# Half of the k-blocks of the second MLP product by Strassen's method, and the first product in three 256-column passes

## The chip, the cores and the metric

The kernel runs on one core of one Trainium2 chip. The metric is the device time of one execution in microseconds (us); the median of the runs counts. The engines are named as the profile names them: PE (TensorE matmuls), PEld (its weight loads), DVE (VectorE), ACT (ScalarE), POOL (GpSimd), SP (the queue that issues the DMAs).

## The reference

256 tokens (SEQ) of width 2048 (D_MODEL) go through two layers. Layer 0 mixes tokens by forgetting attention, layer 1 by a spatial gating unit; behind each stands a channel MLP of width 8192 (D_FF):

```python
def squared_relu_mlp(h, w1, w2):
    a = jax.nn.relu(h @ w1)
    return (a * a) @ w2
...
    for i in range(DEPTH):
        h = rmsnorm(x, g_mix[i])
        ...
        h = rmsnorm(x, g_mlp[i])
        x = x + squared_relu_mlp(h, mlp_w1[i], mlp_w2[i])
```

Everything is float32. The change is in the MLP of both layers.

## The kernel before

Every large product is made of float32r matmuls in three parts: an operand is split into hi (a cast to float32r) and lo (the rest), and hi·hi, hi·lo and lo·hi are added up in PSUM. The activations lie in SBUF as such pairs: H for the input of a product from x, A for the hidden values. The weights come in a stream of half-chunks of [128, 1024] float32 (512 KB), listed in `halves` in the order of use; each is one step of matmul work, listed in `steps`. For each half-chunk SP issues a DMA into `w_stage` (`load`), ACT casts it to `w_hi` (`split_hi`, L65), and DVE subtracts to get `w_lo` (`split_lo`, L73). The order on all engines is written out by hand: in iteration i of the main loop the half-chunk i+8 is loaded, i+4 is cast, i+3 is split, step i is multiplied, and then what `at(i, ...)` has put behind step i is emitted.

The MLP goes in four rounds (c) of 2048 hidden features. A round has two parts:

- The first product, 16 chunks of 128 features (`chunk_w`; the first two in `pair_w`). A chunk is two steps. For each of 16 k-blocks `mm_w` issues two matmuls with weights as the stationary operand: w_hi times H's hi and lo side by side, 512 columns (L122), and w_lo times H's hi, 256 columns (L124). The two halves of the bank are added and squared in `relu2` (L513 on ACT, L514 and L515 on DVE), and split into A (L206 on ACT, L207 on DVE).
- The second product, four units (n) of 512 output columns (`unit_x`), eight steps each. A step has two k-blocks, two blocks of 128 tokens (t) and three parts: 12 matmuls of 512 columns, with A stationary and the weights moving (L107 to L109). `residual` adds the result to x, scaled by r² per token (L220).

PSUM has four banks under the name `acc` and four under `aux`. POOL makes r, the reciprocal root of the norm (L178).

## Time and profile before

| what | value |
|---|---|
| runs | 2141.71, 2141.81, 2142.49 us; median 2141.81 |
| span of the profiled execution, first to last instruction | 2139.4 us, 2.4 below the median of the runs; the page lists no other time for it |
| PE busy | 2130.9 us, 10428 matmuls |
| PE weight loads | 1770.2 us |
| DVE busy | 1232.4 us (58%) |
| ACT busy | 953.2 us (45%) |
| DMA | 399.38 MB, mean 187 GB/s |

Matmul rows overlap, since the end of a matmul is modelled and the next one starts before it: the time that a matmul takes of PE is read from start to start, not from its duration. An instruction on DVE or ACT also starts a little before the one ahead of it has ended where nothing keeps it waiting.

### The profile page before, as it was taken

The page shows a single profiled execution, that of the slowest core. Times are in us where ns is not written, and L with a number is a line of the kernel's source. Part 1 is how long each engine was busy: PE and PEld are TensorE (multiplying, and loading weights), DVE is VectorE, ACT ScalarE, POOL GpSimd, SP SyncE. Part 2 cuts the span into 40 slices and gives each one's busy share as a digit, 9 for nine tenths or more (in the row PEclk, how much of TensorE's full clock was granted, in tenths as well). Part 3 has the DMA queues.
Part 4 walks back from the last instruction along what each step waited for, and adds up shares of the span by engine and source line. Part 5 has one row for each costly group of instructions (what it writes and reads, how often), then busy time and mean ns, then how long its engine had stood idle before and what let it go on. Part 6 is the DMA issues. An engine that isn't in the chain of part 4 may idle for free.

```text
span 2139.4 us, 26750 instructions
## 1 busy us (share of the span) xinstructions
PE 2130.9 (100%) x10428; PEld 1770.2 (83%) x10428; DVE 1232.4 (58%) x1499; ACT 953.2 (45%) x1308; POOL 55.8 (3%) x41
## 2 busy tenths in 40 slices
PE   9999999999999999999999999999999999999999
PEld 6888888888888888888888888888888888888887
DVE  5665665566456456546555676466556655654653
ACT  6535444444344334434454355454434434433442
POOL 1110110000000000000000000000000000000000
PEclk9999999999999999999999999999999999999999
DMA  7555555556656555555556656555555565564563
GB/s 291 187 166 187 157 169 176 179 192 200 197 160 204 187 176 180 195 182 190 189 188 196 210 175 208 174 165 189 197 177 184 191 206 168 184 215 161 188 217 109
DMA packets 111359, 399.38 MB, mean 187 GB/s; under 512 B 12384, under 2 KB 13040, under 8 KB 110848
## 3 DMA queue, kind: packets, MB, share of 16 engines
q1 hardware_dynamic: 109440, 393.40, 56.6%
q0 software_dynamic: 640, 2.17, 0.4%
q10 hardware_dynamic: 1152, 2.10, 0.3%
q8 instruction: 82, 1.34, 0.3%
q14 instruction: 45, 0.37, 0.1%
HBM read 395.50 MB, written 2.11 MB: 186 GB/s over the span
## 4 chain that ended last, share of the span: by engine, by line
PE 98%; DVE 1%; DMA 0%; POOL 0%; ACT 0%; SPq 0%; issue 0%; DVEq 0%; POOLq 0%; ACTq 0%
PE acc L122 25%; PE acc L108 19%; PE acc L107 19%; PE acc L109 19%; PE acc L124 13%; PE aux L239 0%; DMA w_stage<-in_fox_in 0%; PE aux L408 0%; POOL r_qk L178 0%; PE aux L612 0%; PE aux L437 0%; PE aux L486 0%; DVE qk_sq L401 0%; PE aux L476 0%; ACT qk_nat L391 0%; DVE qk_sq L393 0%
## 5 line engine op out<-in xcount | busy, mean ns | idle before, releaser
L73 DVE TENSOR_TENSOR w_lo<-w_stage,w_hi 128x1024 fp32r<-128x1024 f32 (+1 forms) x738 | 875.9, 1224 | 151.1 <-PE acc L108 121.1
L65 ACT CAST w_hi<-w_stage 128x1024 fp32r<-128x1024 f32 (+1 forms) x738 | 747.1, 1046 | 414.0 <-PE acc L109 377.4
L122 PE MATMUL acc<-H,w_hi 128*128 128x512 f32 x2304 | 814.5, 397 | 0.0
L124 PE MATMUL acc<-H,w_lo 128*128 128x256 f32 x2304 | 648.5, 281 | 0.0
L122 PEld LDWEIGHTS acc<-H,w_hi 128*128 128x128 f32 x2304 | 432.5, 188 | 106.7
L107 PE MATMUL acc<-w_hi,A 128*128 128x512 f32 x1280 | 507.3, 396 | 0.0
L108 PE MATMUL acc<-w_lo,A 128*128 128x512 f32 x1280 | 506.2, 395 | 0.0
L109 PE MATMUL acc<-w_hi,A 128*128 128x512 f32 x1280 | 506.1, 395 | 0.0
L124 PEld LDWEIGHTS acc<-H,w_lo 128*128 128x128 f32 x2304 | 434.3, 189 | 0.4
L109 PEld LDWEIGHTS acc<-w_hi,A 128*128 128x128 f32 x1280 | 240.4, 188 | 58.1
L108 PEld LDWEIGHTS acc<-w_lo,A 128*128 128x128 f32 x1280 | 240.5, 188 | 57.4 <-DVE w_lo L73 0.2
L107 PEld LDWEIGHTS acc<-w_hi,A 128*128 128x128 f32 x1280 | 240.5, 188 | 57.5
L107 PE MATMUL acc<-w_hi,H 128*128 128x512 f32 x512 | 206.2, 403 | 0.9 <-ACT w_hi L65 0.9
L108 PE MATMUL acc<-w_lo,H 128*128 128x512 f32 x512 | 202.6, 396 | 0.8 <-DVE gq L709 0.4
L109 PE MATMUL acc<-w_hi,H 128*128 128x512 f32 x512 | 202.2, 395 | 0.0
L513 ACT COPY m_part<-acc 128x256 f32<-128x256 f32 x128 | 47.8, 374 | 286.4 <-PE acc L124 286.4
L514 DVE TENSOR_TENSOR m_a<-acc,m_part 128x256 f32<-128x256 f32 x128 | 54.3, 424 | 208.7 <-ACT m_part L513 208.7
L220 DVE SCALAR_TENSOR_TENSOR x_res<-acc,r_mlp,x_res 128x512 f32<-128x512 f32 (+1 forms) x66 | 46.7, 734 | 213.6 <-PE acc L109 213.6
L107 PEld LDWEIGHTS acc<-w_hi,H 128*128 128x128 f32 x512 | 96.1, 188 | 24.0 <-ACT w_hi L65 1.8
L108 PEld LDWEIGHTS acc<-w_lo,H 128*128 128x128 f32 x512 | 96.1, 188 | 23.8 <-DVE w_lo L73 1.9
L109 PEld LDWEIGHTS acc<-w_hi,H 128*128 128x128 f32 x512 | 96.0, 187 | 23.3
L206 ACT CAST A<-m_a 128x256 fp32r<-128x256 f32 x128 | 52.0, 406 | 121.6 <-DVE m_a L515 121.6
(125 smaller groups left out, 621.0 us busy)
## 6 DMA issues: line engine op xcount, KB each, us to landing
w_stage<-in_w SPq DMA_DIRECT2D x512, 512.0 KB, 4.8
w_stage<-in_fox_in SPq DMA_DIRECT2D x94, 512.0 KB, 5.6
w_stage<-in_fox_out SPq DMA_DIRECT2D x32, 512.0 KB, 4.8
w_stage<-in_sgu_v SPq DMA_DIRECT2D x32, 512.0 KB, 5.0
w_stage<-in_sgu_u SPq DMA_DIRECT2D x32, 512.0 KB, 4.3
w_stage<-in_sgu_out SPq DMA_DIRECT2D x32, 512.0 KB, 4.8
A<-in_xT SPq DMA_DIRECT2D x8, 256.0 KB, 7.8
x_res<-in_x SPq DMA_DIRECT2D x2, 1024.0 KB, 9.2
```

The lines of the kernel that those rows point to most:

```text
L65: self.nc.scalar.copy(out=hi[:, sl], in_=self.staged[i][:, sl])
L73: self.nc.vector.tensor_tensor(out=lo[:, sl], in0=st[:, sl], in1=hi[:, sl].bitcast(F32), op=ALU.subtract)
L107: nc.tensor.matmul(out=acc[t], lhsT=xh, rhs=hi[:, ws], start=(kb == 0), stop=False)
L108: nc.tensor.matmul(out=acc[t], lhsT=xh, rhs=lo[:, ws], start=False, stop=False)
L109: nc.tensor.matmul(out=acc[t], lhsT=xl, rhs=hi[:, ws], start=False, stop=(kb == KB - 1))
L122: nc.tensor.matmul(out=acc, lhsT=hi[:, ws], rhs=o[:, kb, :, :].rearrange("p a s -> p (a s)"), start=(kb == 0), stop=False)
L124: nc.tensor.matmul(out=acc[:, 0:S], lhsT=lo[:, ws], rhs=o[:, kb, 0, :], start=False, stop=(kb == KB - 1))
L206: nc.scalar.copy(out=hi, in_=src)
L220: nc.vector.scalar_tensor_tensor(out=xs, in0=part, scalar=scale[:, t:t + 1], in1=xs, op0=ALU.mult, op1=ALU.add)
L513: nc.scalar.copy(out=part, in_=acc[:, S:2 * S])
L514: nc.vector.tensor_tensor(out=a, in0=acc[:, 0:S], in1=part, op=ALU.add)
```

## The change

1. In the second product, the first 8 of a round's 16 k-blocks (`KS = 8`) are computed for two units at a time by Strassen's method in Winograd's form (`sum_unit`): the operands are cut into quarters (two token blocks by two groups of four k-blocks; two groups of four k-blocks by two units of 512 columns), and seven quarter products take the place of eight. The other 8 k-blocks (`plain`) go as before. Such a unit of 22 steps replaces two `unit_x` of 8 steps: 14 steps are halves of quarter products (6 matmuls), 8 are plain (12 matmuls). In the last round of each layer the units 0 and 1 go that way and 2 and 3 by `unit_x`.
2. The weights' quarters (b11, b12, b21, b22; [128, 2048], 1 MB) are loaded whole, one buffer each, and DVE sums them in place (`sums`, L681): b12 - b11, b22 - b12, b22 - b11, b21 - b22, each just before its product. Each quarter that goes into a product is cast and split anew. The sums of activations (`quarter_sums`, L563 and L567) are made once a round and split into SC.
3. Results are added to x bank by bank (`add_x`, L584), ten additions of [128, 512] for a `sum_unit`; banks Q (of `aux`) and C12 are read while more is still to be added to Q.
4. The first product (`pair_w3`) takes three matmuls of 256 columns for a k-block, all into the same half of a bank: hi·hi, hi·lo, lo·hi. Two chunks share a bank, and the ACT copy of a half falls away. r is put on before the square (`relu2`, L542) through a tile `rb` of r over tokens, made by `token_r` with one float32 matmul; r² in `residual` falls away.
5. Of `w_stage` there are four buffers instead of six; the split runs four steps ahead instead of three.

On PE, at the end of the first product and the start of the second, in the first round. Before:

```order
L122 MATMUL acc<-H,w_hi 128x512
L124 MATMUL acc<-H,w_lo 128x256
L107 MATMUL acc<-w_hi,A 128x512
L108 MATMUL acc<-w_lo,A 128x512
L109 MATMUL acc<-w_hi,A 128x512
```

On PE at the same place now (`aux` is bank Q; the first product is p1, whose first step ends with the sixth matmul):

```order
L513 MATMUL acc<-H,w_hi 128x256
L514 MATMUL acc<-H,w_hi 128x256
L515 MATMUL acc<-H,w_lo 128x256
L605 MATMUL aux<-w_hi,A 128x512
L605 MATMUL aux<-w_lo,A 128x512
L605 MATMUL aux<-w_hi,A 128x512 x2
```

The 512-column matmul of the first product has become two of 256, and the second product's three-part order is kept, with one bank where two took turns.

On DVE, in the second product. Before, from the last split of the first product on:

```order
L207 TENSOR_TENSOR A<-m_a,A 128x256
L73 TENSOR_TENSOR w_lo<-w_stage,w_hi 128x1024 x8
L220 SCALAR_TENSOR_TENSOR x_res<-acc,r_mlp_3417,x_res 128x512 x2
L73 TENSOR_TENSOR w_lo<-w_stage,w_hi 128x1024 x8
L220 SCALAR_TENSOR_TENSOR x_res<-acc,r_mlp_3417,x_res 128x512 x2
```

On DVE now, where the first `sum_unit` of a round passes into the second (b12_4040 is the old content of the buffer b12, b12_4517 the next):

```order
L83 TENSOR_TENSOR w_lo_4497<-b12_4040,w_hi_4478 128x1024
L584 TENSOR_TENSOR x_res_85<-acc_4318,x_res_85 128x512
L584 TENSOR_TENSOR x_res_85<-aux_4453,x_res_85 128x512
L83 TENSOR_TENSOR w_lo_4509<-w_stage_4462,w_hi_4495 128x1024
L83 TENSOR_TENSOR w_lo_4525<-w_stage_4476,w_hi_4507 128x1024
L83 TENSOR_TENSOR w_lo_4541<-b11_4431,w_hi_4523 128x1024
L584 TENSOR_TENSOR x_res_85<-aux_4453,x_res_85 128x512
L681 TENSOR_TENSOR b12_4517<-b12_4517,b11_4431 128x2048
L83 TENSOR_TENSOR w_lo_4553<-b11_4431,w_hi_4539 128x1024
```

Between two pairs of residual additions stood eight splits; now splits, additions and sums of quarters alternate, and three additions and three splits stand between the last use of the old b12 and the sum of the new one.

On SP, at the loads of that second `sum_unit`, now (before, this queue has nothing but `w_stage` loads of 128x1024 there):

```order
L672 DMA b11_4431<-in_w2 128x2048
L61 DMA w_stage_4462<-in_w2 128x1024
L672 DMA b22_4474<-in_w2 128x2048
L61 DMA w_stage_4476<-in_w2 128x1024
L672 DMA b12_4517<-in_w2 128x2048
L672 DMA b21_4519<-in_w2 128x2048
L61 DMA w_stage_4521<-in_w2 128x1024
```

Half of the weights of the second product now come as 1 MB transfers, each of which has to wait until the buffer of its name was last read.

The diff, without docstrings, comments and renamings:

```diff
-STAGE_BUFS = 6
-SPLIT_BUFS = 6
-SPLIT_AHEAD = 3
+STAGE_BUFS = 4
+SPLIT_BUFS = 5
+SPLIT_AHEAD = 4
 LOAD_AHEAD = SPLIT_AHEAD + STAGE_BUFS - 1
+KS = 8
...
     def load(self, i):
-        if i >= len(self.halves) or i in self.staged:
+        if i >= len(self.halves) or i in self.staged or callable(self.halves[i]):
             return
...
+    def sum_up(self, i):
+        for fn in self.sums.get(i, ()):
+            fn()
...
     def split_hi(self, i):
         if i >= len(self.halves):
             return
+        if callable(self.halves[i]):
+            self.staged[i] = self.halves[i]()
...
+    def pair_w3(self, srcs, done, late=False):
...
+                        acc.extend((bank[:, 0:S], bank[:, S:2 * S], bank))
+                for c, a, b in parts:
+                    for kb in range(a, b):
+                        hi, lo = self.split[i + 2 * c + kb // 8]
+                        ws = slice((kb % 8) * P, (kb % 8 + 1) * P)
+                        xh, xl = self.H[:, kb, 0, :], self.H[:, kb, 1, :]
+                        nc.tensor.matmul(out=acc[c], lhsT=hi[:, ws], rhs=xh, start=(kb == 0), stop=False)
+                        nc.tensor.matmul(out=acc[c], lhsT=hi[:, ws], rhs=xl, start=False, stop=False)
+                        nc.tensor.matmul(out=acc[c], lhsT=lo[:, ws], rhs=xh, start=False, stop=(kb == KB - 1))
+            self.steps.append(work)
...
+        def done(acc):
+            if p < KS // 4:
+                a = self.sp.tile([P, 2, S], F32, name=f"raw{p}")
+                self.raw[p] = a
+            else:
+                a = self.tmp.tile([P, 2, S], F32, name="m_a")
+            if len(acc) == 3:
+                nc.vector.tensor_tensor(out=a, in0=acc[2].rearrange("p (b s) -> p b s", s=S), in1=rb2, op=ALU.mult)
+            else:
+                for c in range(2):
+                    nc.vector.tensor_tensor(out=a[:, c, :], in0=acc[c], in1=self.rb, op=ALU.mult)
+            nc.vector.scalar_tensor_tensor(out=a, in0=a, scalar=0.0, in1=a, op0=ALU.max, op1=ALU.mult)
+            self.put_parts(a, self.A[:, 2 * p:2 * p + 2, 0, :], self.A[:, 2 * p:2 * p + 2, 1, :])
+            if KS // 4 <= p < KS // 2:
+                self.quarter_sums(p - KS // 4, a)
...
+    def quarter_sums(self, j, a):
...
+        a11, a21 = self.raw[j][:, :, 0:P], self.raw[j][:, :, P:S]
+        a12, a22 = a[:, :, 0:P], a[:, :, P:S]
+        for n, (u, v, op) in enumerate(((a21, a22, ALU.add), (c[:, 0], a11, ALU.subtract), (a11, a21, ALU.subtract),
+                                        (a12, c[:, 1], ALU.subtract))):
+            nc.vector.tensor_tensor(out=c[:, n], in0=u, in1=v, op=op)
+        o = self.SC[:, :, 2 * j:2 * j + 2, :, :]
+        for n in range(4):
+            nc.scalar.copy(out=o[:, n, :, 0, :], in_=c[:, n])
+            nc.vector.tensor_tensor(out=o[:, n, :, 1, :], in0=c[:, n], in1=o[:, n, :, 0, :].bitcast(F32),
+                                    op=ALU.subtract)
+    def token_r(self, key):
...
+        for t in range(NT):
+            nc.vector.tensor_scalar(out=dg[:, t * P:(t + 1) * P], in0=self.ident, scalar1=r[:, t:t + 1], scalar2=None,
+                                    op0=ALU.mult)
+        ps = self.aux()
+        nc.tensor.matmul(out=ps[:, 0:S], lhsT=self.UO[:, P:2 * P], rhs=dg, start=True, stop=True)
+        nc.scalar.copy(out=self.rb, in_=ps[:, 0:S])
+    def add_x(self, t, n, bank, out=False):
+        xs = self.x[:, t, n * NSL:(n + 1) * NSL]
+        self.nc.vector.tensor_tensor(out=xs, in0=bank, in1=xs, op=ALU.add)
+        if out:
+            self.nc.sync.dma_start(out=self.out[t * P:(t + 1) * P, n * NSL:(n + 1) * NSL], in_=xs)
+    def sum_unit(self, base, u, out):
...
+        def mm(name, lhsT, rhs):
+            if name not in bank:
+                bank[name] = self.aux() if name in "QR" else self.acc()
...
...
+        def triple(name, xh, xl, hi, lo):
+            mm(name, xh, hi)
+            mm(name, xh, lo)
+            mm(name, xl, hi)
+        def product(name, bname, x):
+            for j in range(2):
+                i = len(self.halves)
+                self.halves.append(lambda j=j: quad[bname][:, j * HALF:(j + 1) * HALF])
+                def work(i=i, j=j):
+                    hi, lo = self.split[i]
+                    for k in range(2):
+                        xh, xl = x(2 * j + k)
+                        ws = slice(k * NSL, (k + 1) * NSL)
+                        triple(name, xh, xl, hi[:, ws], lo[:, ws])
+                self.steps.append(work)
+            return len(self.steps) - 1
+        def plain(n, q, h):
+            i = len(self.halves)
+            self.halves.append(w2[base + n * 4 + q][:, h * HALF:(h + 1) * HALF])
+            def work():
+                hi, lo = self.split[i]
+                for k in range(2):
+                    kb = q * 4 + h * 2 + k
+                    ws = slice(k * NSL, (k + 1) * NSL)
+                    for t in range(NT):
+                        ts = slice(t * P, (t + 1) * P)
+                        triple(f"C{t + 1}{n - n0 + 1}", self.A[:, kb, 0, ts], self.A[:, kb, 1, ts], hi[:, ws], lo[:, ws])
+            self.steps.append(work)
+            return len(self.steps) - 1
...
+        def add_on(step, *what):
+            for t, n, name, last in what:
+                self.at(step, lambda t=t, n=n, name=name, last=last: self.add_x(t, n, bank[name], out and last))
+        order = [(n1, 2, 0), (n1, 2, 1), (n1, 3, 0), (n1, 3, 1), (n0, 2, 0), (n0, 2, 1), (n0, 3, 0), (n0, 3, 1)]
+        for name, b, x, key in (("Q", "b11", part(0, 0), "p1"), ("C12", "b22", summed(3), "p3"),
+                                ("C11", "b21", part(half, 0), "p2"), ("Q", "b22", summed(1), "p6"),
+                                ("R", "b11", summed(2), "p7"), ("C21", "b21", part(half, 1), "p4"),
+                                ("Q", "b12", summed(0), "p5")):
+            at[key] = product(name, b, x)
+            at["c" + key] = plain(*order.pop(0))
+        e = plain(*order.pop(0))
+        add_on(at["p1"] + 2, (0, n0, "Q", False))
+        add_on(at["p6"] + 2, (1, n0, "Q", False), (0, n1, "C12", False))
+        add_on(at["p7"] + 2, (1, n1, "C22", False), (1, n1, "R", False))
+        add_on(at["p4"] + 2, (1, n0, "R", False))
+        add_on(e + 1, (0, n1, "Q", True), (1, n1, "Q", True))
+        add_on(e + 2, (0, n0, "C11", True), (1, n0, "C21", True))
+        def load(b, n, q):
+            t = quad[b] = self.sp.tile([P, 2 * HALF], F32, name=b)
+            nc.sync.dma_start(out=t, in_=w2[base + n * 4 + q])
+        for b, n, q, use, free in (("b11", n0, 0, "p1", "p7"), ("b22", n1, 1, "p3", "p6"), ("b12", n1, 0, "p3", "p5"),
+                                   ("b21", n0, 1, "p2", "p4")):
+            at_step = max(at[use] - 1 - SPLIT_AHEAD - 7, self.free.get(b, 0))
+            self.quads.setdefault(at_step, []).append(lambda b=b, n=n, q=q: load(b, n, q))
+            self.free[b] = at[free] - SPLIT_AHEAD + 2
+        def sums(o, x, y, op):
+            return lambda: nc.vector.tensor_tensor(out=quad[o], in0=quad[x], in1=quad[y], op=op)
+        for key, o, x, y in (("p3", "b12", "b12", "b11"), ("p6", "b22", "b22", "b12"), ("p7", "b11", "b22", "b11"),
+                             ("p4", "b21", "b21", "b22")):
+            self.sums.setdefault(at[key] - 1, []).append(sums(o, x, y, ALU.subtract))
+        return e
...
     def mlp(self, l, key, gcol, nkey):
+        w1, w2 = self.ins["w1"], self.ins["w2"]
+        s0 = len(self.steps)
+        self.free = dict.fromkeys(("b11", "b12", "b21", "b22"), s0 + 2)
+        def begin():
+            self.end_mix()
+            self.sp = self.mix()
+            self.raw = {}
+        self.at(s0, begin)
+        self.at(s0 + 2, lambda: self.token_r(key))
         for c in range(4):
             src = [w1[(l * 4 + c) * 16 + j] for j in range(16)]
-            j = 0
-            if c == 0:
-                self.pair_w(src[0:2], "H", [relu2(0), relu2(1)])
-                self.at(len(self.steps) + 2, square_r)
-                j = 2
-            for kb in range(j, 16):
-                self.chunk_w(src[kb], "H", relu2(kb))
-            for n in range(4):
-                def done(acc, step, n=n, c=c):
-                    self.residual(n, acc, self.r2, out=c == 3 and nkey is None)
-                    if c < 3 or nkey is None:
-                        return
-                    self.at(step + 2, self.next_norm(n, step, gcol, nkey))
-                u = ((l * 4 + c) * 4 + n) * 4
-                self.unit_x([w2[u + i] for i in range(4)], "A", done, by_token=nkey is None and c == 3 and n == 3)
-    # ---- layer 1: spatial gating ----
+            for p in range(8):
+                self.pair_w3(src[2 * p:2 * p + 2], self.relu2(p), late=c == p == 0)
+            base = (l * 4 + c) * 16
+            end = c == 3 and nkey is None
+            self.sum_unit(base, 0, end)
+            if c < 3:
+                self.sum_unit(base, 1, False)
+                continue
+            if nkey is not None:
+                e = len(self.steps) - 1
+                for n in range(2):
+                    self.at(e + 3 + n, lambda n=n, e=e: self.at(e + 4 + n, self.next_norm(n, 0, gcol, nkey)))
+            for n in range(2, 4):
+                def done(acc, step, n=n):
+                    self.residual(n, acc, None, out=end)
+                    if nkey is not None:
+                        self.at(step + 2, self.next_norm(n, step, gcol, nkey))
+                u = base + n * 4
+                self.unit_x([w2[u + i] for i in range(4)], "A", done, by_token=end and n == 3)
...
                 while i < len(self.steps) or any(s >= i for s in self.tasks):
                     self.now = i
+                    for fn in self.quads.get(i, ()):
+                        fn()
                     self.load(i + LOAD_AHEAD)
+                    self.sum_up(i + SPLIT_AHEAD + 2)
                     if i + SPLIT_AHEAD < KB // 2:
```

More of the change, by code (lines that the diff above doesn't have):

```diff
@@ L44, in __init__ @@
         self.steps = []
+        self.sums = {}
+        self.quads = {}
         self.tasks = {}
@@ L181, in square_sum @@
     def square_sum(self, ss, t, n):
[L182 removed]
+        junk = self.tmp.tile([P, 2, S], F32, name="m_a").rearrange("p a s -> p (a s)")
         self.nc.scalar.activation(out=junk, in_=self.x[:, t, n * NSL:(n + 1) * NSL], func=AF.Square,
```

109 lines of the change are left out of this document (57 added, 52 removed).

## The prediction

> **What bounds the kernel now.** I read the page first: the span, the busy times, the granted clock by slices and the chain that ended last.
>
> ```profile
> span 2139.4 us, 26750 instructions
> PE 2130.9 (100%) x10428; PEld 1770.2 (83%) x10428; DVE 1232.4 (58%) x1499; ACT 953.2 (45%) x1308; POOL 55.8 (3%) x41
> PEclk9999999999999999999999999999999999999999
> PE 98%; DVE 1%; DMA 0%; POOL 0%; ACT 0%; SPq 0%; issue 0%; DVEq 0%; POOLq 0%; ACTq 0%
> ```
>
> PE is busy throughout, at full clock, and 98% of the chain is its own work. Before, time is the number of matmuls times the spacing of their starts. What matters is how many matmuls go, what spacing the new ones get, and whether DVE, with twice the work per PE time in the new units, still keeps ahead. The next view is the busy time by stage, for one round's first product and then its second.
>
> ```profile
> core 0: us, PE busy (x) PEld busy (x) DVE busy (x) ACT busy (x) POOL busy (x), PEclk, DMA share, GB/s
> 591.30:681.60 90.30, 90.30 (x513) 78.40 (x512) 56.34 (x79) 40.20 (x60) 0.00 (x0) 1.00 0.55 177
> 681.60:771.30 89.70, 89.70 (x386) 72.25 (x385) 43.83 (x42) 36.24 (x36) 0.00 (x0) 1.00 0.61 198
> ```
>
> In the second product, DVE works 43.8 of 89.7 us: 46 us of room a round. Now the spacing of matmuls, from the timeline; columns are start and duration in us.
>
> ```profile
> 600.08 0.40 PE L122 MATMUL acc<-H,w_hi 128*128 128x512 f32 x1
> 600.08 0.19 PEld L124 LDWEIGHTS acc<-H,w_lo 128*128 128x128 f32 x1
> 600.32 0.28 PE L124 MATMUL acc<-H,w_lo 128*128 128x256 f32 x1
> 600.32 0.19 PEld L122 LDWEIGHTS acc<-H,w_hi 128*128 128x128 f32 x1
> 600.44 0.39 PE L122 MATMUL acc<-H,w_hi 128*128 128x512 f32 x1
> ...
> 603.26 0.39 PE L122 MATMUL acc<-H,w_hi 128*128 128x512 f32 x1
> ```
>
> From 600.08 to 603.26 are nine pairs of 512 and 256 columns: 3.18/9 = 353.3 ns a pair. Each weight load starts with the matmul ahead of its own.
>
> ```profile
> 700.60 0.40 PE L107 MATMUL acc<-w_hi,A 128*128 128x512 f32 x1
> 703.40 0.40 PE L107 MATMUL acc<-w_hi,A 128*128 128x512 f32 x1
> ```
>
> These stand twelve matmuls apart, one step of the second product: 2.80/12 = 233.3 ns for 512 columns.
>
> **Term 1, Strassen.** A `sum_unit` has 14 x 6 + 8 x 12 = 180 matmuls of 512 columns where two `unit_x` had 2 x 8 x 12 = 192. There are seven units a layer (two in three rounds, one in the last), 14 in all: 168 matmuls fewer, at 233.3 ns: **-39.2 us**. All of it was on the path.
>
> **Term 2, three passes.** 2 layers x 4 rounds x 16 chunks x 16 k-blocks are 2048 pairs of 353.3 ns that become three matmuls of 256 columns. The columns are as many; only the spacing decides. Bounds from the rows: half of the 512-column spacing, 116.7 ns, gives 350.0 for three, -3.3 x 2048 = -6.7 us. What the 256-column matmul takes of the pair, 353.3 - 233.3 = 120.0, gives 360.0, or +13.7 us. I take the middle, 118.3 ns: 355.0, **+3.5 us**. Nothing hides it. What could spoil it is the weight load, now one for every 256 columns. A stream of short matmuls, each with a load of its own, stands in the spatial gating unit:
>
> ```profile
> 1171.80 1.39 PE L612 MATMUL aux<-wsT,v_sq 128*128 128x128 f32 x11
> L612 PEld LDWEIGHTS aux<-wsT,v_sq x64: 187/192/193, 1171.0 to 1245.7; 128*128 128x128 f32 x64
> L612 PE MATMUL aux<-wsT,v_sq x64: 271/275/275, 1171.2 to 1245.8; 128*128 128x128 f32 x64
> ```
>
> Eleven in 1.39 us with the last one's 0.275 off are 111 ns each, with loads that are shown as 192 ns: loads follow each other at 111 ns or less, under the 116.7 needed. The Trainium skill has a rule against this: TensorE: Matmul & The Clock Gate, "The mechanism", says that a weight load overlaps matmuls in flight only when its row group differs, and every load here is of all 128 rows. By that rule a pass would be its matmul and its load, 118 + 188 = 306 ns, and term 2 would be (918 - 353) x 2048 = +1157 us instead of +3.5; but the pair would already be 353 + 2 x 188 = 729 ns, and the trace has 353.3. By that rule, the trace does not agree.
>
> **Term 3, what DVE must do, and the wait on it.** PE waits for `w_lo`, split four steps ahead. The prices stand in the groups by line (busy us, mean ns of one, idle before) and, for instructions in a row, in the timeline; the 2048 elements are the one row of that size:
>
> ```profile
> L73 DVE TENSOR_TENSOR w_lo<-w_stage,w_hi 128x1024 fp32r<-128x1024 f32 x734 | 873.3, 1226 | 151.1 <-PE acc L108 121.1 <-ACT w_hi L65 23.0 <-issue 4.2
> L65 ACT CAST w_hi<-w_stage 128x1024 fp32r<-128x1024 f32 x734 | 744.8, 1048 | 414.0 <-PE acc L109 377.4 <-DMA w_stage<-in_fox_in 13.0 <-DMA w_stage<-in_w 7.9
> L218 DVE TENSOR_TENSOR x_res<-acc,x_res 128x512 f32<-128x512 f32 x16 | 11.1, 691 | 47.4 <-PE acc L109 47.3
> L515 DVE SCALAR_TENSOR_TENSOR m_a<-m_a 128x256 f32<-128x256 f32 x128 | 54.3, 424 | 4.4
> L564 DVE TENSOR_TENSOR wsT<-wsT,UO x1: 2293/2293/2293, 1084.1 to 1084.1; 128x2048 f32<-128x2048 f32 x1
> 684.07 5.75 DVE L73 TENSOR_TENSOR w_lo<-w_stage,w_hi 128x1024 fp32r<-128x1024 f32 x5
> 409.86 1.39 DVE L218 TENSOR_TENSOR x_res<-acc,x_res 128x512 f32<-128x512 f32 x2 [6.28 <-PE acc L109]
> ```
>
> A split is 1.226 us by itself, but five in a row take 5.75, so 1.131 each where nothing waits; an addition 0.69 to 0.70; a sum of quarters 2.29. Two `sum_unit` of a round take PE 360 x 0.2333 = 84.0 us. In that time DVE has 44 splits, 7 sums (the first of the eight comes earlier), 16 additions (four of the 20 come after) and the first product's last tail (L542, L546, L193 of 512 columns, priced as additions, 2.07): 44 x 1.131 + 7 x 2.29 + 16 x 0.70 + 2.1 = 79.1 us, or 83.1 with 1.226 a split. So DVE is at 94 to 99% of PE: just enough. ACT has 44 x 1.048 = 46 us, no bound. In the first product the tail of two chunks falls from 6 x 0.42 to 3 x 0.69 on DVE; `quarter_sums` adds 16 operations of 256 elements twice a round, spread over four chunks of 45 us with 34 us of DVE idle in 90: hidden, and if the cover went they would cost 16 x 0.43 = 7 us a round.
>
> The one place where DVE stands still is the sum b12 - b11 of the second unit. Its load goes out when the old b12's last split is done; between that and the sum stand three additions and three splits, 3 x 0.70 + 3 x 1.131 = 5.5 us.
>
> ```profile
> w_stage<-in_w SPq DMA_DIRECT2D x512, 512.0 KB, 4.8
> x_res<-in_x SPq DMA_DIRECT2D x2, 1024.0 KB, 9.2
> wsT<-in_sgu_ws SPq DMA_DIRECT2D x1, 1024.0 KB, 7.3
> 5.00:38.00 33.00, 31.36 (x129) 23.43 (x129) 21.30 (x33) 23.86 (x42) 0.52 (x1) 1.00 1.02 390
> ```
>
> The last row, of the start with the DMA engines full, gives 390 GB/s: 512 KB more take 1.34 us, so 1 MB lands after 4.8 + 1.34 = 6.1 us, 7.3 as the load of wsT did among `w_stage` loads, or 9.2 in the queue of the start. DVE is then idle for 0.6, 1.8 or 3.7 us, in each of six pairs. Against it stand 84.0 - 79.1 = 4.9 us of room, or 0.9 with the long split: PE waits from 0 to 3.7 - 0.9 = 2.8 us a pair, 0 to 17 us in all. I take **0**: the load stands among `w_stage` loads, so the 7.3 of wsT is nearest, and splits mostly follow one another, so that 1.8 fits into the room. The loads themselves move the same bytes at 198 GB/s where 390 go; four `w_stage` buffers for six still leave three steps (8.4 us by the 2.80 above) for 4.8 of landing, and in the quarter products no load is needed.
>
> **Term 4, `token_r`.** At the start of each MLP a float32 matmul, two PE records, waits for r, which so far only the residual needed, 40 steps later.
>
> ```profile
> 417.60 1.61 POOL L178 TENSOR_TENSOR r_mlp<-r_mlp_v,mhalf 128x2 f32<-128x2 f32 x1 [120.32 <-DVE r_mlp_v L177]
> 410.36 0.40 PE L122 MATMUL acc<-H,w_hi 128*128 128x512 f32 x1
> 1176.29 0.47 DVE L573 TENSOR_SCALAR diag_r<-ident,r_mix 128x128 f32<-128x128 f32 x2
> ```
>
> r is there at 419.2, the two DVE scalings take 0.47: 419.7. PE reaches the place three steps after 410.36, 24 x 0.3533 = 8.5, plus about 0.9 for eight transposes at the 111 ns above: 419.7. A tie; a split of 1.2 that gets between on DVE makes the wait. The two records (256 columns each, at most 0.23 apart as 512 columns take) are 0.5. So 0.5 to 1.7 us a layer; I take 0.7, in two layers **+1.4 us**. Behind the matmul the whole of PE queues.
>
> **Term 5, the start and layer 0.** The row 5 to 38 us shows PE idle for 1.6 us there. Fewer stage buffers send x a little later, more lead covers waits: -1 to +2, I take **+0.5 us**. r on the other side of the square, the other scratch tile for squares, and the end of the kernel (the last unit is still a `unit_x`) are nothing on PE.
>
> **Sum:** -39.2 + 3.5 + 0 + 1.4 + 0.5 = -33.8 us. The span of 2139.4 becomes 2105.6; the median of the runs is 2.4 above that span, so 2141.8 becomes **2108.0 us**.
>
> **The rivals.**
>
> A. The idle time of DVE at b12 reaches PE. For it: a room of 0.9 us with the long split. Against it: the splits in a row. At 2.8 us in six pairs, +17: 2125.
>
> B. Slower, by a chain through three engines. When DVE has lost its lead, the product after a sum waits for the sum (2.29), the cast of it on ACT (1.05) and the split (1.23): 4.57 us, beside one plain step of 2.80 on PE, so 1.8 us are lost each time, and DVE cannot win its lead back at 99%. In the six second units with four sums each that is 24 x 1.8 = 43 us, 2108 + 43 = 2151. It decides from 33.8/24 = 1.4 us a sum. For it: the three are in a row in the code, and the orders of ACT and DVE leave one split between. Against it: four steps of lead on entering, from a first product where DVE is idle for a third.
>
> C. Slower, by the weight loads. If every pass took the 188 ns that the load of L124 is shown to take, three would take 564 and the total 2108 + 2048 x 0.209 = 2536. It decides from (39.2 - 1.9)/2048 = 18 ns a k-block, a pass of 123.9 instead of 118.3, which is near. Against it: the 111 ns of L612, and that a load already fits beside one 256-column matmul.
>
> ```profile
> L124 PEld LDWEIGHTS acc<-H,w_lo 128*128 128x128 f32 x2304 | 434.3, 189 | 0.4
> ```
>
> The Trainium skill, Perfetto Trace Analysis, "Identifying the Most-Contended Engine", judges the room on TensorE by the busy share of its weight loads and not of its matmuls: by that rule 83% becomes 12312 loads of 1770.2/10428 = 0.1698 us, 2090 of 2106 us or 99%, which speaks for C; but shown loads overlap each other here (192 ns every 111), and the share has no ceiling at 100%.
>
> **How the numbers follow.** My forecast has 0.75, A 0.13, B 0.07, C 0.05. The likeliest gives 2108. Low end: term 2 at -6.7 (10.2 less) and term 5 at -1: 2097. High end: A at 2125, one more for its neighbours, 2126, which leaves out B, C and the worst of term 2 with A. 0.2% is 4.3 us, about what a measurement can tell from no change. Forecast and A are faster, 0.88, of which I give 0.02 to their far end within 0.2%: faster 0.86, same 0.02; B and C make slower 0.12.
>
> **What would show it.** Right: in the second product 2904 matmuls of 512 columns at 233 ns; the three lines of `pair_w3` start 117 to 120 ns apart; the two `sum_unit` of a round in 84 to 85 us with DVE over 90% busy there; waits of PE on `w_lo` of a few us in all. Wrong: pairs of units of 87 us or more, with waits of PE on `w_lo` L83 and of ACT on the sums L681 (B), of DVE on the DMA of b (A), or 256-column spacings over 124 ns (C).

## The result and the profile after

The changed kernel takes 2110.84 us (median; 2110.66 to 2111.15), the kernel before on the same chip 2141.82 (2141.71 to 2142.49): a ratio of 0.9852, 95% interval 0.9838 to 0.9866. The forecast was 2108.0 in a range of 2097 to 2126. The span fell from 2139.4 to 2108.5 us, by 30.9.

The first lines of the page of the changed kernel, the span, the busy times and the granted clock:

```profile
span 2108.5 us, 30777 instructions
PE 2098.4 (100%) x12312; PEld 1837.9 (87%) x12312; DVE 1517.0 (72%) x1663; ACT 1016.0 (48%) x1266; POOL 56.0 (3%) x41
PEclk9999999999999999999999999999999999999999
```

PE is the bound as before; DVE has gone from 1232 to 1517 us. Next the busy times by stage, for one first product and the second product behind it (columns as in the same view of before):

```profile
589.80:680.60 90.80, 90.80 (x769) 90.80 (x768) 62.68 (x75) 40.41 (x48) 0.00 (x0) 1.00 0.64 226
680.70:764.60 83.90, 83.90 (x362) 67.42 (x361) 77.65 (x70) 45.26 (x45) 0.00 (x0) 1.00 0.46 162
```

PE has no idle time in either. DVE stands at 77.65 of 83.90 us in the second product, 93%. The timeline of PE in the first product, and at the matmul of `token_r` (L579) in its first round, with DVE's rows and POOL's row (it makes r) ahead of that matmul:

```profile
639.85 0.28 PE L513 MATMUL acc<-H,w_hi 128*128 128x256 f32 x1
639.97 0.28 PE L514 MATMUL acc<-H,w_hi 128*128 128x256 f32 x1
640.08 0.28 PE L515 MATMUL acc<-H,w_lo 128*128 128x256 f32 x1
...
641.98 0.28 PE L513 MATMUL acc<-H,w_hi 128*128 128x256 f32 x1
```

```profile
422.21 0.28 PE L515 MATMUL acc<-H,w_lo 128*128 128x256 f32 x1
422.93 0.67 PE L579 MATMUL aux<-m_part,UO 128*128 128x256 f32 x2 [0.44 <-DVE m_part L576]
423.25 0.47 PE L513 MATMUL acc<-H,w_hi 128*128 128x256 f32 x1
```

```profile
419.94 0.17 DVE L163 TENSOR_SCALAR r_mlp_v<-tot_mlp 128x2 f32<-128x2 f32 x1
420.02 2.36 DVE L83 TENSOR_TENSOR w_lo<-w_stage,w_hi 128x1024 fp32r<-128x1024 f32 x2
422.30 0.47 DVE L576 TENSOR_SCALAR m_part<-ident,r_mlp 128x128 f32<-128x128 f32 x2
420.20 1.61 POOL L164 TENSOR_TENSOR r_mlp<-r_mlp_v,mhalf 128x2 f32<-128x2 f32 x1 [119.94 <-DVE r_mlp_v L163]
```

From 639.85 to 641.98 are 18 passes, 118.3 ns each. L579 starts 0.72 us after the pass ahead of it instead of 0.12, because DVE does two splits before the scalings (L576); r is there at 421.81 already. Put together, the 30.9 us are, all from start to start of PE's matmuls in the two traces:

| stage | before | after | difference in the kernel |
|---|---|---|---|
| two `unit_x` / one `sum_unit`, 14 times | 44.8 | 42.0 | -39.2 |
| first product, each of 8 rounds | 90.45 | 90.88 | +3.4 |
| `token_r`, first round of each layer, beyond that | 0.85 | 1.98 | +2.3 |
| start of the first MLP | 410.36 | 412.93 | +2.6 |

### The profile page after: what moved, and what is told of

The parts are those of the page before. It is cut to its first block, busy times and chain, and to the rows that moved or that the text cites. A ratio compares the mean times of both kernels' runs of the same rounds, so it can differ in the third digit from the quotient of the medians.

```text
span 2108.5 us, 30777 instructions
## 1 busy us (share of the span) xinstructions
PE 2098.4 (100%) x12312; PEld 1837.9 (87%) x12312; DVE 1517.0 (72%) x1663; ACT 1016.0 (48%) x1266; POOL 56.0 (3%) x41
## 5 line engine op out<-in xcount | busy, mean ns | idle before, releaser
L83 DVE TENSOR_TENSOR w_lo<-w_stage,w_hi 128x1024 fp32r<-128x1024 f32 (+1 forms) x626 | 755.0, 1224 | 265.3 <-ACT w_hi L75 93.3
L75 ACT CAST w_hi<-w_stage 128x1024 fp32r<-128x1024 f32 (+1 forms) x626 | 647.4, 1047 | 563.4 <-DMA w_stage<-in_w 176.5
L513 PE MATMUL acc<-H,w_hi 128*128 128x256 f32 x2048 | 576.0, 281 | 0.0
L514 PE MATMUL acc<-H,w_hi 128*128 128x256 f32 x2048 | 575.3, 281 | 0.0
L514 PEld LDWEIGHTS acc<-H,w_hi 128*128 128x128 f32 x2048 | 385.9, 188 | 0.4
L513 PEld LDWEIGHTS acc<-H,w_hi 128*128 128x128 f32 x2048 | 385.9, 188 | 0.4
L605 PE MATMUL acc<-w_hi,A 128*128 128x512 f32 x1120 | 363.2, 395 | 0.0
L75 ACT CAST w_hi<-b 128x1024 fp32r<-128x1024 f32 x196 | 198.6, 1046 | 139.9 <-DVE b L681 104.8
L605 PEld LDWEIGHTS acc<-w_hi,A 128*128 128x128 f32 x1120 | 209.9, 187 | 51.4
L83 DVE TENSOR_TENSOR w_lo<-b,w_hi 128x1024 fp32r<-128x1024 f32 x196 | 235.6, 1216 | 1.4 <-issue 1.4
L605 PE MATMUL acc<-w_lo,A 128*128 128x512 f32 x560 | 221.2, 395 | 0.0
L117 PE MATMUL acc<-w_hi,A 128*128 128x512 f32 x384 | 152.8, 398 | 0.0
L119 PE MATMUL acc<-w_hi,A 128*128 128x512 f32 x384 | 151.7, 395 | 0.0
L118 PE MATMUL acc<-w_lo,A 128*128 128x512 f32 x384 | 151.7, 395 | 0.0
L681 DVE TENSOR_TENSOR b<-b,b 128x2048 f32<-128x2048 f32 x56 | 127.8, 2282 | 0.0
L605 PEld LDWEIGHTS acc<-w_lo,A 128*128 128x128 f32 x560 | 105.0, 187 | 25.7
```

Of the source, the lines that this page charges most:

```text
L75: self.nc.scalar.copy(out=hi[:, sl], in_=self.staged[i][:, sl])
L83: self.nc.vector.tensor_tensor(out=lo[:, sl], in0=st[:, sl], in1=hi[:, sl].bitcast(F32), op=ALU.subtract)
L117: nc.tensor.matmul(out=acc[t], lhsT=xh, rhs=hi[:, ws], start=(kb == 0), stop=False)
L118: nc.tensor.matmul(out=acc[t], lhsT=xh, rhs=lo[:, ws], start=False, stop=False)
L119: nc.tensor.matmul(out=acc[t], lhsT=xl, rhs=hi[:, ws], start=False, stop=(kb == KB - 1))
L513: nc.tensor.matmul(out=acc[c], lhsT=hi[:, ws], rhs=xh, start=(kb == 0), stop=False)
```

## The experiments

All ratios below are to the kernel before, run on the same chip beside it.

**The costs without the gain.** Every round's second product goes back to four `unit_x`, the rest of the change stays.

```diff
-KS = 8
+KS = 0
-            self.sum_unit(base, 0, end)
-            ...
+            for n in range(4):
+                ...
+                self.unit_x([w2[u + i] for i in range(4)], "A", done, ...)
```

> No Strassen: all four units of a round as before, but the three 256-column passes, r before the square, four stage buffers and four steps of lead. Theory: what is left are the costs alone, 3.4 us of passes, 2.3 of the float32 matmul of r and 2.6 of the start; span 2139.4 + 8.3 = 2147.7 us, so 39.2 us more than the whole change. Rival: part of the gain comes from the lead and the r before the square: span 2139 or less.

Measured 2149.76 us, 1.0033 (1.0021 to 1.0044); span 2148.2. Rounds of the first product take 90.88 us, second products 89.6, and the MLP starts at 413.4. So the three passes, `token_r` and the start alone cost 8.8 us of span, and the units of Strassen's form bring 2148.2 - 2108.5 = 39.7 against the 39.2 that their matmuls are worth: nothing of the gain is lost on the way (the other 0.5 us is this run's later start).

**The sum that waits for its load (b12).** The prediction has DVE stand still at this sum. In the changed kernel it does not. Its timeline:

```profile
541.40 0.68 DVE L584 TENSOR_TENSOR x_res<-aux,x_res 128x512 f32<-128x512 f32 x1
542.04 2.29 DVE L681 TENSOR_TENSOR b<-b,b 128x2048 f32<-128x2048 f32 x1
```

and the transfers of the quarters, all 56 of them (KB each, median us to landing):

```profile
b<-in_w SPq DMA_DIRECT2D x56, 1024.0 KB, 8.6
```

This load was issued at 535.4 and landed at 542.01, just ahead of the sum. The six loads of this kind took 5.7 to 7.1 us, less than the median of all 56, and from their issue to the sum were 6.5 to 7.6 us, so that none of the six sums waits. The experiment issues the load two iterations later still:

```diff
-            self.free[b] = at[free] - SPLIT_AHEAD + 2
+            self.free[b] = at[free] - SPLIT_AHEAD + (4 if b == "b12" else 2)
```

> The load of b12 for the second unit of a round is issued two iterations later, behind the 1 MB load of b21, so it lands some 2.6 us later and DVE stands still for that time before the sum b12 - b11, in six pairs. Theory (DVE is idle 6.3 of 83.9 us of a pair and four steps ahead): PE does not notice, span 2108.5 within 1 us. Rival A (DVE's idle time there passes to PE): 6 x 2.6 = 15.6 us, span 2124. Rival B (the lead is lost and each sum makes PE wait 1.8 us): up to 40 us, span 2148.

Measured 2111.47 us, 0.9854 (0.9839 to 0.9868), as the changed kernel. Now DVE does wait; from the table of waits (us in total, times, longest):

```profile
DVE b L681 <- DMA b<-in_w: 14.0, 6, 3.3
```

Pairs of units take 84.36, 84.0, 84.0, 84.0, 84.08 and 84.3 us: of these 14.0 us, 0.7 reach PE in the whole kernel. The lead of four steps covers that wait, and the rivals that let it reach PE (A, and B behind it) fall for this kernel.

**How much room DVE has.** Two or four operations of 512 elements without use behind each sum:

```diff
                 nc.vector.tensor_tensor(out=quad[o], in0=quad[x], in1=quad[y], op=op)
+                for k in range(2):        # 4 in the other
+                    w = self.tmp.tile([P, 2, S], F32, name="m_a")...
+                    nc.vector.tensor_tensor(out=w, in0=self.x[:, 0, 0:NSL], in1=self.x[:, 1, 0:NSL], op=op)
```

> The changed kernel with two more VectorE operations of 512 elements behind each of the eight sums of a pair of units (their result is not used). At about 0.6 us each (a split of 1024 elements takes 1.22) they add 9.6 us to the 77 that VectorE is busy in a pair of units, 87 for TensorE's 84.0. Theory (VectorE's few per cent of room and its lead of four steps are what hides the sums): the 3 us that are missing come mostly out of the lead, 0 to 3.3 us lost a pair, 2111 to 2134 in all. Rival (VectorE has no reserve; every operation put ahead of a split reaches TensorE): 9.6 a pair, 2178.

> The same with four more operations behind each sum: 19.2 us a pair of units, VectorE at 96 for TensorE's 84.0. Theory: VectorE becomes the bound of the units; the lead of at most four steps (about 8 us) gives some of the 12 back, so 4 to 12 us lost a pair and half of that in each of the two single units, 2139 to 2195 in all. Rival (TensorE still hides it): 2111.

With two, 2151.89 us, 1.0042 (1.0028 to 1.0056); with four, 2219.66, 1.0359 (1.0345 to 1.0373). Both are above their ranges; I had priced an operation at 0.6 us. The groups by line of DVE in one pair of units, with two:

```profile
L685 DVE TENSOR_TENSOR m_a<-x_res 128x512 f32<-128x512 f32 x14 | 9.0, 686 | 0.0
L83 DVE TENSOR_TENSOR w_lo<-w_stage,w_hi 128x1024 fp32r<-128x1024 f32 x18 | 21.8, 1219 | 3.5 <-ACT w_hi L75 3.5
```

and the busy times of that pair with two and of one with four:

```profile
687.23:778.33 91.10, 85.92 (x362) 66.86 (x361) 84.87 (x83) 42.88 (x44) 0.00 (x0) 1.00 0.42 145
```

```profile
696.80:797.09 100.29, 90.11 (x362) 70.40 (x361) 94.96 (x99) 44.28 (x45) 0.00 (x0) 0.95 0.40 140
```

At 0.69 us each, 16 operations are 11.0 us and 32 are 22.0; these pairs grew from 84.0 to 91.1 and 100.3, by 7.1 and 16.3. Over the six pairs the growth is 5.6 to 7.1 us with two operations and 14.9 to 17.2 with four. So of the 11.0 us, 3.9 to 5.4 a pair stayed hidden and the rest reached PE. With four, the hidden part can't be read off: the granted clock of 0.95 has a part in that pair, where PE runs at half the clock three times, for 3.4 us each. Nor do the two runs show at which amount PE loses its first time. DVE is shown busy for 93% of the pair of 91.1, and 3.5 us of the rest are waits for ScalarE's casts (L75). The extra operations do not delay the cast of a sum, which starts at 710.17, right behind a sum that ends at 710.06; they stand on DVE ahead of the split that follows it. So the chain sum, cast, split of rival B takes part, beside the amount on DVE. With two of them, the gain of the whole change is gone.

**The other first product.** Strassen's units stay, but the first product goes back to 512 and 256 columns a k-block, with a tail of ScalarE copies and, on DVE, two additions, a multiplication and the square:

```diff
-                        nc.tensor.matmul(out=acc[c], lhsT=hi[:, ws], rhs=xh, ...)   # three passes
-                        ...
+                        self.mm_w(i + 2 * c + kb // 8, acc[c], kb, "H")
...
+                nc.scalar.copy(out=part, in_=acc[c][:, S:2 * S])
+                nc.vector.tensor_tensor(out=a[:, c, :], in0=acc[c][:, 0:S], in1=part, op=ALU.add)
+            nc.vector.tensor_tensor(out=a, in0=a, in1=rb2, op=ALU.mult)
             nc.vector.scalar_tensor_tensor(out=a, in0=a, scalar=0.0, in1=a, op0=ALU.max, op1=ALU.mult)
```

> Strassen stays, the first product goes back to one matmul of 512 and one of 256 columns a k-block, with the ACT copy of the second half of each bank and six instead of three DVE operations for a pair of chunks. Theory: the three passes cost 90.88 - 90.45 = 0.43 us a round in the traces, 3.4 us in eight rounds, and DVE has room for the tail; the span falls from 2108.5 to 2105.1 us, rounds of the first product to 90.45. Rival: the passes cost nothing by themselves and the longer tail takes DVE's lead into the units: rounds of 90.9 and pairs of units over 84.0 us, span 2108.5 or more.

Measured 2119.28 us, 0.9885 (0.9869 to 0.9902), slower than the changed kernel. The theory's span of 2105.1 is a miss. The rival had the units right, whose pairs take 85.4 to 88.2 and the singles 45.9 and 43.6, 19.7 us lost in all, but neither had the rounds: the six later ones are faster than in either kernel, 88.75 us. ScalarE shows the place, its timeline at the end of a first product:

```profile
668.14 2.00 ACT L75 CAST w_hi<-w_stage 128x1024 fp32r<-128x1024 f32 x2
676.04 1.05 ACT L75 CAST w_hi<-w_stage 128x1024 fp32r<-128x1024 f32 x1 [5.90 <-DMA w_stage<-in_w]
677.00 1.05 ACT L75 CAST w_hi<-b 128x1024 fp32r<-128x1024 f32 x1
677.95 0.64 ACT L534 COPY m_part<-acc 128x256 f32<-128x256 f32 x2
680.59 0.62 ACT L192 CAST A<-m_a 128x512 fp32r<-128x512 f32 x1 [2.00 <-DVE m_a L537]
```

My reading is a ring, in which each lap makes the next one late: the cast of the result (L192) stands 2.00 us waiting for DVE's last operation, with the casts of weights queued behind it; DVE's splits come late, so the `w_stage` buffers come free late, the next load goes out late, and ScalarE waits for it, 5.90 us here. When the unit begins at 683.9, PE waits on the split:

```profile
686.46 0.50 PE L596 MATMUL aux<-w_lo,A 128*128 128x512 f32 x1 [0.74 <-DVE w_lo L83]
693.36 0.50 PE L596 MATMUL acc<-w_lo,SC 128*128 128x512 f32 x1 [1.03 <-DVE w_lo L83]
```

So is it the amount on DVE or the order in the queues? Two things were changed, first together and then each alone. `light`: two additions and one operation of 512 (relu and the factor) on DVE, the square on ScalarE, and the split of the result one step later. `late`: only the split later. `short`: only the smaller tail.

```diff
-            nc.vector.tensor_tensor(out=a, in0=a, in1=rb2, op=ALU.mult)
-            nc.vector.scalar_tensor_tensor(out=a, in0=a, scalar=0.0, in1=a, op0=ALU.max, op1=ALU.mult)
+            nc.vector.scalar_tensor_tensor(out=a, in0=a, scalar=0.0, in1=rb2, op0=ALU.max, op1=ALU.mult)   # light, short
+            nc.scalar.activation(out=a, in_=a, func=AF.Square)
-            self.put_parts(a, ...)
+            self.at(self.now + 1, rest)        # light, late: put_parts and quarter_sums in rest
```

> Strassen as in the changed kernel; the first product goes back to a 512-column and a 256-column pass for each k-block, but its tail is kept short on VectorE: ScalarE copies one half and squares, VectorE adds two halves of 256 and does one operation of 512 (relu and the factor per token), and the split into two parts is put one step later. Theory (two things: the two passes run at 346.7 ns a k-block when nothing disturbs them, against 355 for three passes; and what the other run of this form lost in the units was VectorE's lead, eaten by its longer tail): rounds of the first product 88.75 instead of 90.88, units at 84.0, so 17 us faster than the changed kernel, 2094. Rival 1 (any tail with a copy by ScalarE makes the splits late): units lose 15 to 20, 2110 to 2119. Rival 2 (the pace of the first product is 353.3 as in the kernel before): rounds 90.45, 2107.

> Strassen with the 512 and 256-column passes and the long tail of the first such run (ScalarE copies; on VectorE two additions of 256, one multiplication and one relu-and-square of 512), and only the split of the result put one step later. Theory (it is the order that counts: ScalarE's cast of the result waits for VectorE's last operation with the casts of the weights queued behind it, 2.0 us each time; put later, that wait goes and the ring of loads, casts and splits keeps its lead): units back at 84 to 85 us a pair, 2099 to 2104. Rival (it is the amount on VectorE, 0.7 us more a pair of chunks): units as in the first run, 85.4 to 88.2, 2113 to 2120.

> The counterpart: the short tail on VectorE (two additions of 256 and one operation of 512, the square on ScalarE), with the split of the result where it was, in the same step. The theory of the order: ScalarE still waits in line for VectorE, for its square and its cast, so units stay late, 2108 to 2120. The rival, the amount on VectorE: units at 84 to 85, 2099 to 2104.

| split of the result | long tail on DVE | short tail on DVE |
|---|---|---|
| same step | 2119.28, 0.9885 (0.9869 to 0.9902) | 2117.37, 0.9883 (0.9868 to 0.9898) |
| one step later | 2100.57, 0.9805 (0.9789 to 0.9821) | 2099.43, 0.9797 (0.9784 to 0.9810) |

It is mainly the order. With the split a step later all pairs of units are back at 84.0 us (84.06 once), whatever the tail; with the short tail alone they take 84.4 to 87.0. Added up in the four traces, the units lose 19.7 us with the long tail in the same step, 14.7 with the short one, and nothing a step later. That the total of `short` is hardly better than that of the long tail comes from three of its later rounds, which take 90.44 us and not 88.75 (below). What `light` was expected to show, that the longer tail eats the lead, is a miss; the 17 us that it was to bring came to 11.4, since the first rounds do not have the faster pace (below) and the start is 3.8 us later. The tables of waits (us in total, times, longest) show how long ScalarE waits for the loads: first the kernel with the long tail in the same step, then `late`.

```profile
ACT w_hi L75 <- DMA w_stage<-in_w: 245.9, 103, 6.5
```

```profile
ACT w_hi L75 <- DMA w_stage<-in_w: 123.6, 69, 6.0
```

What in that order costs the lead is not shown to the end. The cast of the result waits for DVE in the changed kernel as well, as long in all as in the kernel with the long tail; first the changed kernel, then that one:

```profile
ACT A L192 <- DVE m_a L546: 115.6, 47, 3.3
```

```profile
ACT A L192 <- DVE m_a L537: 116.3, 48, 5.3
```

In the changed kernel no unit loses time by it. So this wait alone does not break the ring. The two kernels differ in ScalarE's copies, in the tail on DVE and in the spacing of the passes, and which of these makes the same order harmful was not taken apart.

`light` and `late` beat the changed kernel and the kernel before.

**Two paces of the same pairs.** The rounds of 88.75 us come from the spacing on PE. The timeline of `light` in its second round, and in its first:

```profile
639.94 0.39 PE L132 MATMUL acc<-H,w_hi 128*128 128x512 f32 x1
640.28 0.39 PE L132 MATMUL acc<-H,w_hi 128*128 128x512 f32 x1
...
643.40 0.39 PE L132 MATMUL acc<-H,w_hi 128*128 128x512 f32 x1
```

```profile
449.79 0.40 PE L132 MATMUL acc<-H,w_hi 128*128 128x512 f32 x1
450.15 0.39 PE L132 MATMUL acc<-H,w_hi 128*128 128x512 f32 x1
...
453.32 0.40 PE L132 MATMUL acc<-H,w_hi 128*128 128x512 f32 x1
```

Ten pairs take 3.46 us in the one and 3.53 in the other, with the same instructions: 346.7 ns each, or 345 and 361 in turn. In `light` the first round of a layer starts at 346.7 and changes where eight transposes (L225) come in between; the later rounds are back at 346.7. A unit in between does not always end the slower pace: `lightfix` (below) keeps it in its second round, and `short` has it in three later rounds. The kernel before had 353.3 in all its rounds. The experiment lets the 256-column pass go first in every second k-block:

```diff
+        if turn:        # kb % 2
+            nc.tensor.matmul(out=acc[:, 0:S], lhsT=lo[:, ws], rhs=o[:, kb, 0, :], ...)
+            nc.tensor.matmul(out=acc, lhsT=hi[:, ws], rhs=o[:, kb, :, :]..., ...)
+            return
```

> As the last one, but in every second k-block of the first MLP product (not of the gating product, which stays as a control) the 256-column pass goes ahead of the 512-column one. In the traces so far these pairs run at 346.7 ns in some stretches and at 353.3 in others (345 and 361 in turn), with the same instructions. Theory (the pace hangs on how passes of two widths follow each other): with half as many changes of width each way it shows one pace in all rounds, 350 ns, rounds of 89.6 us where the last one has 88.75 or 90.45. Rival (it is set by the state in which the round begins, whatever the order): the same 346.7 or 353.3, changing where transposes or another product came between, and no difference in time against the last kernel by more than 3 us.

Measured 2105.11 us, 0.9825 (0.9812 to 0.9839), against 2099.35 for the kernel without the turn. All six later rounds take 89.94 us, 351.3 ns a pair, and the first ones 91.50 where they had 91.93 to 91.95: one pace, as the order of widths would have it. The gating product of the same run, whose order was left alone, still has both: 346.7 ns a pair from 1215 us on, and 353.3 from 1231 on. That the pace hangs on how widths follow each other is shown; what puts PE into the slower one is not.

**The two waits.** Three tries at the waits for `token_r` and for the gate's weights in layer 0 (`fox_f`, split into f_parts, multiplied at L299). First, on the changed kernel, L579 one step later and the gate two steps earlier:

```diff
-        self.at(s0 + 2, lambda: self.token_r(key))
+        self.at(s0 + 3, lambda: self.token_r(key))
-        self.at(3, self.fox_f)
+        self.at(1, self.fox_f)
```

> Two waits of PE that the change brought are taken away: the float32 matmul of r stands one step later (after step 3 instead of 2 of an MLP), and the small load of the forget gate's weights is issued before x instead of behind it. Theory: PE waited 0.6 us for r in each of two layers and 1.35 us at 38.8 us for the gate's operand; 2.5 us go, span 2106.0. The two records of the matmul itself stay. Rival: what waits there is only moved, x lands later and the first use of its norm waits: span 2107.2 (1.3 less) or no change.

Measured 2115.19 us, 0.9871 (0.9856 to 0.9886), slower than the changed kernel by 4, which neither the theory nor the rival had. L579 waits as long as before, since one step later another split stands ahead of the scalings and itself waits for PE. DVE's timeline there:

```profile
428.88 1.23 DVE L83 TENSOR_TENSOR w_lo<-w_stage,w_hi 128x1024 fp32r<-128x1024 f32 x1 [1.61 <-PE acc L515]
430.03 0.48 DVE L576 TENSOR_SCALAR m_part<-ident,r_mlp 128x128 f32<-128x128 f32 x2
```

And the gate's product now waits longer. Its row on PE, and the busy times around it:

```profile
35.41 3.20 PE L299 MATMUL aux<-H,f_parts 128*32 128x512 f32 x7 [3.40 <-DVE f_parts L193]
```

```profile
34.00:42.00 8.00, 6.59 (x17) 2.93 (x18) 3.90 (x5) 2.94 (x5) 0.00 (x0) 0.57 0.79 272
```

Behind 3.4 us of waiting the granted clock is 0.57 on average, and matmuls follow each other at 427 ns instead of 233. The Trainium skill, TensorE: Matmul & The Clock Gate, "Part 1: The HAM clock gate", says that the array's clock halves after an idle window of about 3.4 us. The traces agree in kind: behind a gap of 3.8 us from start to start here the clock is at half for 6.8 us, and behind gaps of 3.1 in `light` and 3.4 in `best` (below) for 3.4 us; behind 1.6 in the changed kernel and 2.2 in `lightfix` it is not. In length they differ from it, and the measurement decides: 2.7 us in `pace` and 2.3 in the run with four operations on DVE were enough, while that same run has gaps of 2.8 us behind which the clock stays. What besides the length decides, the traces don't show.

Second, on `light`: the scalings one step ahead of L579 instead, and the gate's product one step later (`lightfix`). Third, the gate's weights loaded two steps earlier, with its split and products where they were (`best`).

```diff
+        self.at(s0 + 1, lambda: self.scale_r(key))        # both: the two scalings, taken out of token_r
         self.at(s0 + 2, lambda: self.token_r(key))
-        self.at(self.now + 6, products)
+        self.at(self.now + 7, products)        # lightfix
-        self.at(3, self.fox_f)
+        self.at(1, self.fox_f)        # best, with parts, products and by_token two steps later
```

> As the kernel with the short tail, and two waits of the changed kernel mended: the scaling for the factors per token is put one step ahead of its product (so VectorE does it ahead of a split, not behind two), and the gate's product one step later (so its weights have landed). Theory: TensorE's 0.60 us ahead of each of the two products of the factors goes, and the 1.35 us at 38.8 us of the layer's start, 2.5 us less than the kernel with the short tail, 2091 by its theory. Rival (what the wait hid comes out at the next place, as when the product was moved one step later): no change against the kernel with the short tail.

> As the kernel with the short tail (2099.4 us, 0.9797 of the kernel before), with the two waits mended in another way: the scaling for the factors per token one step ahead of its product, and the gate's weights loaded two steps earlier while their split and products stay where they are. Theory: the 0.6 us ahead of each of the two products of the factors goes (1.2 us), and so does the 2.85 us wait for the gate's weights at 41.0 us together with the slow matmuls behind it (about 1.5 us): 5 us less at most, ratio 0.9775, 2094.5 us. Rival (the start is bound by its transfers, and the wait comes out at the next split): 1.2 us less, ratio 0.979.

`lightfix`: 2100.76 us, 0.9803 (0.9789 to 0.9816). `best`: 2099.35, 0.9794 (0.9780 to 0.9807). Neither is told from `light`. The scalings do what they should: the first rounds go from 92.39 to 91.95 us, and L579 starts 0.30 after the pass ahead of it where it was 0.75. The gate is the rival's case twice: in `lightfix` the wait comes out later, 1.9 us at 56.1 and 1.4 at 61.2; in `best` it is still there, 3.1 us at 41.1. The reason is in ScalarE's timeline:

```profile
36.66 1.05 ACT L75 CAST w_hi<-w_stage 128x1024 fp32r<-128x1024 f32 x1 [5.36 <-DMA w_stage<-in_fox_in]
37.94 1.04 ACT L75 CAST w_hi<-w_stage 128x1024 fp32r<-128x1024 f32 x1 [0.23 <-PE acc L118]
39.22 1.04 ACT L75 CAST w_hi<-w_stage 128x1024 fp32r<-128x1024 f32 x1 [0.24 <-DMA w_stage<-in_fox_in]
40.18 0.40 ACT L192 CAST f_parts<-scores 128x256 fp32r<-128x256 f32 x1
```

The gate's weights had landed long before; their cast stands behind three casts of `w_stage`, the first of which waits 5.36 us for its transfer. What the start waits for there is the stream of transfers through the four `w_stage` buffers, and not the one load.

## Why the prediction was right, step by step

**Term 1 (-39.2)** is exact: each `sum_unit` takes 42.0 us, and L605 to L605 is 233.3 ns on average.

**Term 2 (+3.5)** measured +3.4. The passes stand 118.3 ns apart, the middle of the two bounds. No row spoke for the middle rather than for a bound, so that it was met this closely is luck. Rival C, which needed 123.9, falls: weight loads of 188 ns shown at every 118 cover one another. What the term did not see is that its reference, 353.3 ns a pair, was the slower of two paces, though the trace of before has both. Its timeline in the gating product shows ten pairs in 3.46 us:

```profile
1235.09 0.39 PE L122 MATMUL acc<-H,w_hi 128*128 128x512 f32 x1
...
1238.55 0.39 PE L122 MATMUL acc<-H,w_hi 128*128 128x512 f32 x1
```

Against 346.7 the passes cost 2048 x 8.3 ns = 17 us. They are not free, they only look so beside the kernel before.

**Term 3 (0)** is right in its result, and the sum of DVE's work was near: 79.1 us a pair were forecast with back-to-back splits, and 77.65 and 76.92 are shown. Its picture of the wait was not right. DVE was to stand still for 1.8 us at the sum with b12, and stands still for none: 6.5 to 7.6 us passed there where 5.5 were reckoned, for DVE waits for a cast on the way, and the loads took 5.7 to 7.1 us where 7.3 was taken. What idle time DVE has in a pair is mostly for ScalarE's casts, 4.8 us in the second product shown above:

```profile
L83 DVE TENSOR_TENSOR w_lo<-w_stage,w_hi 128x1024 fp32r<-128x1024 f32 x19 | 23.0, 1217 | 4.9 <-ACT w_hi L75 4.8
```

That a wait at b12 would have been hidden is shown by the later load of b12. The place for rival B exists, though, and it is near: with 11 us more on DVE a pair, behind the sums, PE loses 6 to 7 of them, and the run with four operations ends far behind the kernel before.

**Term 4 (+1.4)** is mis-sized: +2.3. The tie at 419.7 itself came out, with both sides 2.6 us later: r was there at 421.81, so that the scalings could have ended at 422.28, and PE came to the place at 422.33. The step that failed is the price of a split that gets between on DVE, named and taken at 0.2 a layer: two of them, 2.36 us, hold the scalings back, and the wait is 0.60 a layer, beside 0.5 for the two records. The bound of 1.7 a layer held (1.13).

**Term 5 (+0.5)** is mis-sized, and outside its bounds of -1 to +2: +2.6. The five runs whose code is the same up to the MLP start it 2.3 to 3.0 us later than the one trace of before. The step that failed took the start for one that more lead covers. In the trace, PE's matmuls stand 427 ns apart until 11.1 us where the kernel before was at full pace from 6.5 (1.4 us), and the gate's product waits 1.35 us at 38.8. The run with the later b12, whose code is the same up to there, was at full pace from 6.6, but waited 1.4 us for a split at 20.7 and started the MLP at 412.7: so the slow clock is not what decides. What stays is less load-ahead in the start, which is argued and not shown: no run puts the old number of buffers back. The kernels with the other first product start their MLP another 3 to 5 us later, with the same code up to 40 us. On PE that is the gate's product, which waits 2.7 to 4.0 us in `s512`, `light`, `late` and `short`, and the 3.4 us at half the clock behind it, which cost about 1.5. Why the product waits longer there stays open; their traces differ from about 10 us on in when the first transfers land.

Terms 4 and 5 together are 3.0 of the 2.9 us by which the span was missed.

The Trainium skill, TensorE: Matmul & The Clock Gate, "The mechanism", has weight loads overlap matmuls in flight only across row groups. That does not hold for these loads, as the row of L612 had said: loads shown as 188 ns stand behind passes that start every 118.3. The Trainium skill, Perfetto Trace Analysis, "Identifying the Most-Contended Engine", takes the busy share of weight loads for the room of TensorE. By it the prediction reckoned 99% for the kernel after. The page of the profile has 87%, at a PE without idle time, and PE's spacing is as forecast without it. The share tells nothing of the bound here.

## What to carry to other kernels

Price a change of matmul shapes by start-to-start spacing in more than one stretch of the trace: the same pairs ran at 346.7 and at 353.3 ns. When DVE goes from 49% to 93% of a stage, as in the second product here, what decides is the order in the queues of ScalarE and DVE, not only the amount: putting the split of the result one step later was worth 15 to 20 us in the units of the kernels with the other first product, and the shorter tail on DVE by itself 5, by one trace of each. Look for a cast that waits for the other engine's last operation, since it holds every cast behind it; but whether that costs the lead has to be tried, for the changed kernel has such waits and loses nothing. A single wait moved earlier or later comes out again at the next place unless the queue that it stands in is looked at first.

## What the runs showed of the hardware that was not expected

- Pairs of a 512 and a 256-column float32r matmul have two paces on PE, 346.7 ns, or 345 and 361 ns in turn, with the same instructions; with the order turned in every second pair there is one, 351.3. Three passes of 256 columns have one, 355.0.
- PE is at 427 ns for 512 columns at the start, and again while the granted clock is at half, for 3.4 us (6.8 once). That came behind some gaps of 2.3 to 4.2 us from start to start, and did not behind others of up to 2.8; behind 2.2 and less the spacing stayed at 233.
- A weight load that is shown as 188 ns fits into passes of 118 ns without a gap.
